# Six output-gate chunks moved from the scan stage into the seven-product stage, with a later start and a denser spread of the scan's steps

## The chip, the core and the metric

The kernel runs on one core of a Trainium2 chip. Its engines are TensorE (PE; its weight loads are PEld), VectorE (DVE), ScalarE (ACT), GpSimd (POOL) and SyncE (SP), whose queue issues every DMA here. The metric is the device time of one execution, in microseconds.

## What is computed

One step of a hybrid decoder layer over 576 tokens: 512 of a new prompt and 64 of eight running sequences. All is float32.

```
h = RMSNorm_pre(x)
[q|k|v|z_a|xBC|z_s|dt|g_a|g_s] = h @ w_in
A: sliding-window attention on q, k, v, times silu(z_a)
B: causal conv + SiLU on xBC, chunked state-space scan, gated norm with silu(z_s)
merged = sigmoid(g_a) * (A @ w_attn_br) + sigmoid(g_s) * (B @ w_ssm_br)
x <- x + RMSNorm_post(merged @ w_out)
```

The change concerns the two gates `g_a` and `g_s`, each of 2048 features. They are needed only at the very end (`merged`), so their products with `w_in` can stand anywhere before that.

## The kernel before

Activations are held transposed: 16 tiles of 128 features by 576 tokens, each as a high and a low part (`XH`, `XL`), so that one float32 product is three matmuls of 288 columns (`xh,wh`, `xl,wh`, `xh,wl`). A chunk is 128 output features. Its weights are two units of 128x1024 (tile `wr`). `split_w` (L329, L330) turns a unit into `wh` (a cast on ACT) and `wl` (a subtraction on DVE). `wr`, `wh` and `wl` have three buffers each.

A chunk is computed in one of two ways. `dense` (L345, its matmuls are L365) takes 16 k-tiles x 2 halves x 3 = 96 matmuls. `Strassen` takes chunks in pairs: seven products of 8 x 3 = 24 matmuls, 168 for a pair where `dense` has 192, with four additions of weight units on DVE and seven splits in place of four. Its matmuls are L164 to L166.

The stages stand in this order:

- 2b: the projections for z_a, z_s and xBC as pairs. The list `ch` gives the chunks, `pairs` joins them two by two.
- 3: `dense` chunks for k, v, q. The attention runs beside them in the background.
- 4: `dense` chunks for the gates. The scan (branch B) runs beside them in the background.
- 5: the two branch products and the output product, four `dense` chunks and then pairs in each phase.
- 6: the rest of the output product and the final norm.

Background work is a Python generator; each `yield` ends a step. `dense` calls `pump` 16 times in a chunk, each time adding `self.rate` to a credit, and runs one step for each whole credit. In stage 4 the rate is `R4` = 1.08, so a chunk carries 17.28 steps. `master` in stage 4 goes through eight groups of the scan. In each, `prompt(g)` (four pieces of 128 tokens: `d_front`, `d_back`), `sample(g)` (the 64 sample tokens: `e_front`, `e_back`) and `tail(g - 1)` (the gated norm of the group before, `d_norm`) are interleaved step by step. A group has 60 steps.

Code order is not the order on an engine. The framework's scheduler places each engine's instructions by its own model of when they can start, earlier code first, so scan steps that are late in code order come ahead of chunks that are ready. Stage 4's pools also take over memory of stage 3's, so the first load of the scan waits until the attention's last store has left.

Two small pieces of the scan are touched as well. In `e_front` eight ACT instructions (L1393) form relu(a - x) for eight heads, each 64x64. In `e_stack` ACT casts one operand twice to two partition ranges (L1405 and L1406, L1410 and L1411).

Of the kernel before, what the change touches and what calls it, by code (L numbers as in the profile page):

```python
# [13 lines left out]
AF = mybir.ActivationFunctionType  # L14
ALU = mybir.AluOpType
# [3 lines left out]
P = 128  # L19
# [3 lines left out]
TS = 64  # L23
T = TP + TS
TH = T // 2
# [6 lines left out]
SG = 8  # L32
# [5 lines left out]
Z_A, Z_S, G_A, G_S, KK, VV, QQ, XBC = 0, 16, 48, 64, 80, 84, 88, 104  # L38
# [54 lines left out]
NZ0 = 6  # L93
L_CV = 3 + TP + 11 * NB
HK = UK // 2
R4 = 1.08
NB0 = 4
NO1 = 12
TSP = 384
# [169 lines left out]
class Prog:  # L269
# [188 lines left out]
    def run(self):  # L458
        nc, io, tc = self.nc, self.io, self.tc
# [7 lines left out]
        for jj in range(4):  # L467
            for c in [KK + jj, VV + jj] + [QQ + 4 * jj + i for i in range(4)]:
                pl += win(c)
        for c in list(range(G_A, G_A + 16)) + list(range(G_S, G_S + 16)):  # L470
            pl += win(c)
        units = lambda w, c: [io[w][2 * c], io[w][2 * c + 1]]
        for w, o in (("wat", 0), ("wss", 0), ("wss", 16), ("wo", 0)):
# [269 lines left out]
    def stage2b(self, s2):  # L743
        nc, io = self.nc, self.io
# [9 lines left out]
        def z_out(dst):  # L754
# [7 lines left out]

            return dest, fin

        def conv_out(m):
            def dest():
                s = self.t(p, (P, L), "cs", bufs=2)
# [35 lines left out]
        ch = []  # L803
# [3 lines left out]
            ch.append((Z_S + c, z_out(self.d_zs[c])))  # L807
        for m in range(NCONV):
            ch.append((XBC + m, conv_out(m)))
        w = io["win"]  # L810
        pairs = []
        for (a, ea), (b, eb) in zip(ch[0::2], ch[1::2]):
# [88 lines left out]
    def stage3(self, s3):  # L901
# [97 lines left out]
        for jj in range(4):  # L999
            self.dense(k_evac(jj), raw=self.raw)  # L1000
            self.dense(v_evac(jj), raw=self.raw)
            for h in range(2):
# [3 lines left out]
                    if h == 0 and c == 0:  # L1006
                        v_tail(jj)
                ready[0] = j + 1
        for c in range(2):
            self.dense(self.g_evac(self.d_ga[c]), raw=self.raw)  # L1010
        self.drain()

# [159 lines left out]
    def stage4(self, s4):  # L1172
# [18 lines left out]
        def tail(g):  # L1191
            if g >= 0:
                yield from self.d_norm(g)
            if g + 2 < SG:
                self.group_load(g + 2)
            yield

        def master():
            self.G, self.AT, self.E2 = {}, {}, {}
            self.group_load(0)  # L1200
            self.at_load(0, 0)
            self.ats_load(0)
            yield
            for g in range(SG):
                a = prompt(g)
                yield from rr([a, sample(g), a, tail(g - 1)])
            yield from tail(SG - 1)

        self.bg.append(master())
        self.rate = R4  # L1210
        for c in range(2, 16):
            self.dense(self.g_evac(self.d_ga[c]), raw=self.raw)
        for c in range(15):
            self.dense(self.g_evac(self.d_gs[c]), raw=self.raw)
        p = self.p4
        first = self.t(p, (P, 4, T), "xs", bufs=2)
# [13 lines left out]

        for k in range(6):
            load(k)
        self.dense(self.g_evac(self.d_gs[15]), hook=take, raw=self.raw)
        self.drain()

    def group_load(self, g):
# [119 lines left out]
    def e_front(self, g, st):  # L1356
# [31 lines left out]
        nc.vector.tensor_mul(cbm[0:TS, 0:TS], cb[0:TS, 0:TS], self.bdt)  # L1388
        bts = st["bts"] = self.t(p, (TS, P), "bts", bufs=1)
        nc.scalar.copy(bts, cb[0:TS, P : 2 * P])  # L1390
        for i in range(8):
            ah = self.at[0:TS, 4, h8.start + i : h8.start + i + 1]
            nc.scalar.activation(ats[:, i], ats[:, i], AF.Relu, bias=ah, scale=-1.0)  # L1393
        nc.scalar.activation(ats, ats, AF.Exp, scale=-1.0)
        yield
        nc.vector.tensor_tensor(ats, ats, cbm[0:TS, 0:TS].unsqueeze(1).broadcast_to([TS, 8, TS]), ALU.mult)
# [2 lines left out]
    def e_stack(self, u, st):  # L1399
        nc, p = self.nc, self.p4  # L1400
        us = slice(32 * u, 32 * u + 32)
        xdf = st["xdes"].rearrange("p h d -> p (h d)")
        bts = st["bts"]
        x3 = self.t(p, (96, TP), "x3", F32R, bufs=2)
        nc.scalar.copy(x3[0:32], xdf[us])  # L1405
        nc.scalar.copy(x3[32:64], xdf[us])  # L1406
        nc.vector.tensor_sub(x3[64:96], xdf[us], x3[us].bitcast(F32))
        b3 = self.t(p, (96, P), "b3", F32R, bufs=1)
        other = slice(32 - 32 * u, 64 - 32 * u)
        nc.scalar.copy(b3[us], bts[us])  # L1410
        nc.scalar.copy(b3[64:96], bts[us])  # L1411
        nc.vector.tensor_sub(b3[other], bts[us], b3[us].bitcast(F32))
        bm = self.t(p, (96, 4, P), "bm", F32R, bufs=2)
        nc.vector.tensor_tensor(
            bm,
            b3.bitcast(F32).unsqueeze(1).broadcast_to([96, 4, P]),
            self.bm.unsqueeze(2).broadcast_to([96, 4, P]),
            ALU.mult,
        )
        return x3, bm  # L1420
# [447 lines left out]
```

## Time and profile before

| | |
|---|---|
| median of three runs | 3005.59 us (3004.52 to 3009.65) |
| the profiled execution | 3007.05 us, of which the span of the trace is 3005.3 us |
| PE busy | 2916.9 us (97%) |
| DVE busy | 2181.9 us (73%) |
| ACT busy | 1575.8 us (52%) |
| POOL busy | 347.1 us (12%) |
| mean granted TensorE clock | 0.990 |

A table of windows gives, for each stretch of the span, the time in which each engine had an instruction running, the number of instructions in brackets, the granted clock as a share of full speed, and how busy the DMA engines were. Matmuls overlap in the trace, so the time of one in a row of matmuls is the stretch divided by their count, not the duration shown for one.

### The profile page before, as it was taken

To read this page: it belongs to the slowest core of one execution; us is meant where nothing else is said; L and a number is where in the kernel's file an instruction comes from. 1 tells how busy PE (TensorE), PEld (TensorE's weight loads), DVE (VectorE), ACT (ScalarE), POOL (GpSimd) and SP (SyncE) were. 2 spreads that over 40 slices of the span, in tenths; PEclk is the share of its full clock that TensorE was granted. 3 is DMA by queue.
4 is the path that set the end of the run, shared out by engine and by line. 5 is a ranking of instruction groups with operands and counts; after the bars stand their busy time and mean duration, and the time that the engine had idled before them with its cause. 6 is when DMAs were issued, how large, how long until landed. Compare 5 with 4: busy or idle time off the path is not lost. (4 is left out here: it accounts for less than half of the span.)

```text
span 3005.3 us, 56009 instructions
## 1 busy us (share of the span) xinstructions
PE 2916.9 (97%) x21696; PEld 2829.8 (94%) x21696; DVE 2181.9 (73%) x3224; ACT 1575.8 (52%) x3163; POOL 347.1 (12%) x431
## 2 busy tenths in 40 slices
PE   8999999999999999999999699999999999999998
PEld 7999999999999999999999488888899999999997
DVE  7866666688888885666654887766767687887865
ACT  4444444455555554555555766666544454544552
POOL 1000000000000001322221443333200000000002
PEclk9999999999999999999999899999999999999998
DMA  8733333343433433333334677767675485775836
GB/s 288 245 127 126 114 128 123 117 131 114 128 126 115 136 112 115 100 100 99 97 104 157 199 238 244 248 237 234 210 242 179 156 284 179 253 236 165 261 116 237
DMA packets 233755, 512.23 MB, mean 170 GB/s; under 512 B 46857, under 2 KB 79369, under 8 KB 233233
## 3 DMA queue, kind: packets, MB, share of 16 engines
q1 hardware_dynamic: 233488, 508.66, 51.6%
q8 instruction: 170, 2.79, 0.4%
q14 instruction: 97, 0.79, 0.1%
HBM read 402.97 MB, written 109.65 MB: 171 GB/s over the span
## 5 line engine op out<-in xcount | busy, mean ns | idle before, releaser
L365 PE MATMUL pd<-xh,wh 128*128 128x288 f32 (+1 forms) x2464 | 738.1, 301 | 5.2 <-DVE raw L579 2.7
L365 PE MATMUL pd<-xl,wh 128*128 128x288 f32 (+1 forms) x2464 | 730.8, 297 | 0.0
L365 PE MATMUL pd<-xh,wl 128*128 128x288 f32 (+1 forms) x2464 | 730.5, 297 | 0.0
L164 PE MATMUL pb<-xh,wh 128*128 128x288 f32 x1608 | 476.2, 296 | 5.2 <-ACT wh L329 4.4
L166 PE MATMUL pb<-xh,wl 128*128 128x288 f32 x1608 | 476.0, 296 | 3.8 <-DVE wl L330 3.8
L365 PEld LDWEIGHTS pd<-xh,wh 128*128 128x128 f32 (+1 forms) x2464 | 460.9, 187 | 19.9 <-issue 9.1
L165 PE MATMUL pb<-xl,wh 128*128 128x288 f32 x1608 | 475.4, 296 | 0.0
L365 PEld LDWEIGHTS pd<-xl,wh 128*128 128x128 f32 (+1 forms) x2464 | 461.7, 187 | 9.8 <-issue 6.0
L365 PEld LDWEIGHTS pd<-xh,wl 128*128 128x128 f32 (+1 forms) x2464 | 461.5, 188 | 6.9 <-issue 4.8
L330 DVE TENSOR_TENSOR wl<-wr,wh 128x1024 fp32r<-128x1024 f32 (+1 forms) x276 | 336.4, 1221 | 156.1 <-ACT wh L329 150.5
L329 ACT CAST wh<-wr 128x1024 fp32r<-128x1024 f32 (+1 forms) x276 | 283.3, 1029 | 242.5 <-PE pb L165 106.7
L329 ACT CAST wh<-sx 128x1024 fp32r<-128x1024 f32 x198 | 207.8, 1050 | 282.7 <-PE pb L165 156.8
L329 ACT CAST wh<-sr 128x1024 fp32r<-128x1024 f32 x170 | 178.6, 1050 | 318.0 <-PE pb L165 240.4
L164 PEld LDWEIGHTS pb<-xh,wh 128*128 128x128 f32 x1608 | 303.1, 189 | 6.2 <-ACT wh L329 4.8
L166 PEld LDWEIGHTS pb<-xh,wl 128*128 128x128 f32 x1608 | 303.1, 188 | 4.6 <-DVE wl L330 4.6
L165 PEld LDWEIGHTS pb<-xl,wh 128*128 128x128 f32 x1608 | 303.3, 189 | 0.0
L330 DVE TENSOR_TENSOR wl<-sr,wh 128x1024 fp32r<-128x1024 f32 x170 | 208.0, 1224 | 109.0 <-ACT wh L329 108.9
L330 DVE TENSOR_TENSOR wl<-sx,wh 128x1024 fp32r<-128x1024 f32 x198 | 241.6, 1221 | 58.4 <-ACT wh L329 58.1
L164 PE MATMUL pb<-T2h,wh 128*128 128x288 f32 x536 | 158.2, 295 | 4.1 <-ACT k L173 4.1
L164 PE MATMUL pb<-T1h,wh 128*128 128x288 f32 x536 | 158.5, 296 | 0.9 <-ACT wh L329 0.8
L165 PE MATMUL pb<-T3l,wh 128*128 128x288 f32 x536 | 158.5, 296 | 0.0
L164 PE MATMUL pb<-T3h,wh 128*128 128x288 f32 x536 | 158.4, 295 | 0.0
(345 smaller groups left out, 6488.6 us busy)
## 6 DMA issues: line engine op xcount, KB each, us to landing
wr<-win SPq DMA_DIRECT2D x192, 512.0 KB
sr<-win SPq DMA_DIRECT2D x112, 512.0 KB
sr<-dso SPq DMA_DIRECT2D x64, 288.0 KB
wr<-wss SPq DMA_DIRECT2D x34, 512.0 KB
att<-dat SPq DMA_DIRECT2D x32, 512.0 KB
s<-sst SPq DMA_DIRECT2D x32, 512.0 KB
o_ss<-s SPq DMA_DIRECT2D x32, 512.0 KB
sr<-wss SPq DMA_DIRECT2D x30, 512.0 KB
```

Source lines behind the costliest of these rows:

```text
L164: mm(ps, a, xh, start=k == 0 and not cont, stop=False, skip_group_check=cont)
L165: mm(ps, a, xl, start=False, stop=False, skip_group_check=cont)
L166: mm(ps, b, xh, start=False, stop=k == UK - 1, skip_group_check=cont)
L329: nc.scalar.copy(wh[:, o : o + n], raw[:, o : o + n])
L330: nc.vector.tensor_sub(wl[:, o : o + n], raw[:, o : o + n], wh[:, o : o + n].bitcast(F32))
L365: self.nc.tensor.matmul(ps[x], wt[:, sl], xt[k][:, xs], start=k == 0 and s == 0, stop=k == KC - 1 and s == 2)
```

## The change

Three things are altered. The last six chunks of `g_s` (`NGS` = 6) leave stage 4 and the list of dense weight units; they become the last three pairs of stage 2b, with an output routine `g_out` that stores the raw product. Stage 3 ends with four chunks of `g_a` (`NG3`) where it had two. Stage 4 thus has 22 chunks where it had 30; `R4` becomes 1.49 (23.84 steps a chunk), the loads of the second group are issued with those of the first, the scan begins with ten empty steps, and in the first group the place of the norm is taken by 14 empty steps. In `e_front` and `e_stack` work goes from ACT to POOL.

```
-R4 = 1.08
+NGS = 6
+R4 = 1.49
+NG3 = 4
...
-        for c in list(range(G_A, G_A + 16)) + list(range(G_S, G_S + 16)):
+        for c in list(range(G_A, G_A + 16)) + list(range(G_S, G_S + 16 - NGS)):
             pl += win(c)
...
+        def g_out(dst):
+            def dest():
+                raw = self.t(self.rp, (P, T), "raw", bufs=2)
+                return raw, raw[:, 0:TH], [(raw[:, TH:T], slice(0, TH), same)]
+
+            def fin(raw):
+                self.st(dst, raw)
+                yield
+
+            return dest, fin
...
             ch.append((XBC + m, conv_out(m)))
+        for c in range(16 - NGS, 16):
+            ch.append((G_S + c, g_out(self.d_gs[c])))
...
-        for c in range(2):
+        for c in range(NG3):
             self.dense(self.g_evac(self.d_ga[c]), raw=self.raw)
         self.drain()
...
             if g >= 0:
                 yield from self.d_norm(g)
-            if g + 2 < SG:
+            else:
+                for _ in range(14):
+                    yield
+            if 0 <= g < SG - 2:
                 self.group_load(g + 2)
             yield
...
             self.ats_load(0)
-            yield
+            self.group_load(1)
+            for _ in range(10):
+                yield
...
-        for c in range(2, 16):
+        for c in range(NG3, 16):
             self.dense(self.g_evac(self.d_ga[c]), raw=self.raw)
-        for c in range(15):
+        for c in range(15 - NGS):
             self.dense(self.g_evac(self.d_gs[c]), raw=self.raw)
...
-        self.dense(self.g_evac(self.d_gs[15]), hook=take, raw=self.raw)
+        self.dense(self.g_evac(self.d_gs[15 - NGS]), hook=take, raw=self.raw)
...
-        for i in range(8):
-            ah = self.at[0:TS, 4, h8.start + i : h8.start + i + 1]
-            nc.scalar.activation(ats[:, i], ats[:, i], AF.Relu, bias=ah, scale=-1.0)
+        nc.gpsimd.tensor_tensor(
+            ats, self.at[0:TS, 4, h8].unsqueeze(2).broadcast_to([TS, 8, TS]), ats, ALU.subtract
+        )
+        nc.scalar.activation(ats, ats, AF.Relu)
...
-        nc.scalar.copy(x3[32:64], xdf[us])
+        nc.gpsimd.tensor_copy(x3[32:64], x3[0:32])
...
-        nc.scalar.copy(b3[64:96], bts[us])
+        nc.gpsimd.tensor_copy(b3[64:96], b3[us])
```

The order of instructions moves in three places. The first is PE at the start of the scan, about 40 gate matmuls behind its first transpose. L1330 (L1350 in the changed kernel) is the scan's first state product; L365 (L367) is a gate matmul; L1348, L1451, L1454, L1284 and L1322 are scan matmuls. Before:

```order
L365 MATMUL pd_19990<-xh_58_395,wl_19999 128x288
L1330 MATMUL pb_18830<-xde_18695,bt_18737 128x512
L1294 MATMUL pb_18847<-C_18666,B_18665 128x128
L1295 MATMUL pb_18847<-cst_72,B_18665 128x128
L1348 MATMUL pb_18871<-att_18673,xdt_18693 64x128 x8
L1451 MATMUL pb_18918<-sh_18892,cm_18648 128x512
L1454 MATMUL pb_18926<-x_2690_18882,bm_18890 128x512
L1284 MATMUL pb_18942<-cst_72,xs_18664 128x128 x4
L1322 MATMUL pb_18971<-C_18666,S_18832 128x128 x4
```

The rows go on like this, without one gate matmul, through the whole first group and the first half of the second. The same place in the changed kernel:

```order
L367 MATMUL pd_20366<-xh_44_367,wl_20375 128x288
L1350 MATMUL pb_19757<-xde_19649,bt_19691 128x512
L1314 MATMUL pb_19776<-C_19575,B_19574 128x128
L1315 MATMUL pb_19776<-cst_72,B_19574 128x128
L367 MATMUL pd_20367<-xh_44_367,wh_20374 128x288
L367 MATMUL pd_20367<-xl_45_368,wh_20374 128x288
L367 MATMUL pd_20367<-xh_44_367,wl_20375 128x288
L367 MATMUL pd_20366<-xh_46_371,wh_20374 128x288
```

Gate matmuls now stand between the scan's in the whole first group: from the first transpose to the norm of that group PE meets 236 of them, where it met 44 before.

The second place is DVE in the middle of stage 4, where L330 (L332) is the subtraction that finishes a weight unit and every other row is the scan's. Before, two such rows have eight others between them:

```order
L330 TENSOR_TENSOR wl_22148<-wr_21878,wh_22147 128x1024
L1488 TENSOR_TENSOR xs_21036<-xs_21036,z_22028 128x576
L1407 TENSOR_TENSOR x_3199_22103<-xdes_21930,x_3199_22103 32x512
L1297 TENSOR_TENSOR cbm_22062<-pb_22059,cst_72 128x128
L1407 TENSOR_TENSOR x_3221_22220<-xdes_21930,x_3221_22220 32x512
L1311 TENSOR_TENSOR att_21895<-att_21895,cbm_22062 128x512 x2
L1412 TENSOR_TENSOR b_3200_22107<-bts_21984,b_3200_22107 32x128
L1351 TENSOR_TENSOR xs_21880<-pb_22092,xs_21880 128x4x128
L1414 TENSOR_TENSOR bm_22111<-b_3200_22107,cst_72 96x512
L330 TENSOR_TENSOR wl_22288<-wr_22040,wh_22287 128x1024
```

In the changed kernel, at the start of the second group:

```order
L332 TENSOR_TENSOR wl_21093<-wr_20837,wh_21092 128x1024
L1488 TENSOR_TENSOR xdes_20240<-pb_20231,xdes_20240 64x512
L1371 TENSOR_TENSOR xs_19573<-pb_20247,xs_19573 128x4x128
L1502 TENSOR_TENSOR xs_19573<-pb_20290,xs_19573 128x4x64
L1306 TENSOR_TENSOR xdt_20314<-pb_20309,dt_13566 128x512
L1308 TENSOR_TENSOR xde_20316<-pb_20309,dec_13600 128x512
L1509 TENSOR_TENSOR xs_19573<-xs_19573,z_20243 128x576
L1509 TENSOR_TENSOR xs_19573<-xs_19573,z_20245 128x576
```

The next such row in the changed kernel is the 49th behind the one shown. Five of the eight groups have a stretch of this kind, 36 to 49 rows long.

## Rows read from the trace of the kernel before

**Rows 1.** Windows of stage 4: length, busy of each engine, clock, DMA share, GB/s.

```profile
1640.00:2190.00 550.00, 509.02 (x3671) 441.39 (x3670) 404.80 (x592) 350.51 (x900) 192.02 (x143) 0.98 0.69 231
1640.00:1740.00 100.00, 70.50 (x438) 51.57 (x437) 80.93 (x121) 74.73 (x205) 39.12 (x31) 0.88 0.69 217
1740.00:2190.00 450.00, 438.52 (x3236) 389.82 (x3235) 323.87 (x472) 275.78 (x695) 152.90 (x113) 1.00 0.69 234
```

**Rows 2.** Windows of the gate matmuls alone (L365): length, PE, PEld, clock, DMA share.

```profile
1640.00:1740.00 100.00, 18.14 (x116) 15.95 (x115) 0.88 0.69 217
1740.00:2190.00 450.00, 325.82 (x2094) 290.33 (x2093) 1.00 0.69 234
```

**Rows 3.** Windows of 20 us at the start of the scan, columns as in rows 1.

```profile
1640.00:1660.00 20.00, 12.88 (x95) 11.18 (x94) 11.44 (x20) 18.24 (x54) 0.92 (x1) 0.89 1.04 335
...
1700.00:1720.00 20.00, 13.49 (x73) 8.09 (x73) 16.66 (x26) 17.74 (x47) 11.39 (x9) 0.83 0.27 86
1720.00:1740.00 20.00, 17.66 (x118) 14.77 (x119) 16.50 (x21) 10.47 (x25) 9.13 (x7) 1.00 0.80 227
```

**Rows 4.** Waits of PE from 1636 to 1760 us: total, times, longest.

```profile
PE pb L1330 <- ACT bt L1299: 10.2, 1, 10.2
PE pb L1451 <- ACT sh L1432: 6.7, 2, 5.4
```

**Rows 5.** Timeline of SP's queue at the start of the scan: start, duration, what is issued.

```profile
1628.07 0.33 SPq L292 DMA_DIRECT2D wr<-win  x1
...
1634.60 0.33 SPq L292 DMA_DIRECT2D B<-dxc  x1
...
1654.78 1.69 SPq L292 DMA_DIRECT2D wr<-win  x2
...
1737.25 0.40 SPq L292 DMA_DIRECT2D wr<-win  x1
```

**Rows 6.** Timeline of PE: the scan's first transpose, and stage 5's first seven-product matmul.

```profile
1640.65 0.27 PE L1284 MATMUL pb<-cst,xs 128*128 128x128 f32 x1
...
2268.90 0.29 PE L164 MATMUL pb<-xh,wh 128*128 128x288 f32 x1
```

**Rows 7.** Windows of stage 2b, columns as in rows 1.

```profile
300.00:325.00 25.00, 25.00 (x191) 25.00 (x190) 17.45 (x17) 11.49 (x16) 0.00 (x0) 1.00 0.34 121
...
1100.00:1125.00 25.00, 25.00 (x191) 25.00 (x190) 18.50 (x28) 15.51 (x33) 0.20 (x2) 1.00 0.32 110
```

**Rows 8.** Groups of DVE by line, 1640 to 2190 us: busy, mean ns, idle before.

```profile
L330 DVE TENSOR_TENSOR wl<-wr,wh 128x1024 fp32r<-128x1024 f32 x46 | 59.2, 1287 | 52.9 <-ACT wh L329 52.9
L1311 DVE TENSOR_TENSOR att<-att,cbm 128x512 f32<-128x512 f32 x64 | 53.8, 865 | 11.7 <-ACT att L1305 10.8
L1433 DVE TENSOR_TENSOR sl<-s,sh 128x512 fp32r<-128x512 f32 x64 | 53.4, 842 | 8.0 <-ACT sh L1432 4.5 <-PE pb L1348 3.4
```

**Rows 9.** One line of DVE each: ns shortest/median/longest, starts.

```profile
L1311 DVE TENSOR_TENSOR att<-att,cbm x48: 676/684/1920, 1761.3 to 2158.0; 128x512 f32<-128x512 f32 x48
...
L1433 DVE TENSOR_TENSOR sl<-s,sh x64: 673/681/2111, 1658.3 to 2158.6; 128x512 fp32r<-128x512 f32 x64
```

**Rows 10.** A group of POOL, 1640 to 2190 us, columns as in rows 8.

```profile
L1436 POOL TENSOR_TENSOR s<-s,es 128x512 f32<-128x512 f32 x64 | 75.0, 1175 | 158.4 <-DVE sl L1433 151.1 <-DMA e<-de 6.5 <-DMA o_ss<-s 0.8
```

**Rows 11.** Groups of ACT, 1640 to 2190 us, columns as in rows 8.

```profile
L1393 ACT ACTIVATE ats<-ats,at 64x64 f32<-64x64 f32 x64 | 17.3, 337 | 23.5 <-DMA ats<-dats 19.7 <-PE pb L1284 3.8
...
L1406 ACT CAST x<-xdes 32x512 fp32r<-32x512 f32 x16 | 9.9, 618 | 0.3
...
L1394 ACT ACTIVATE ats<-ats 64x512 f32<-64x512 f32 x8 | 5.0, 624 | 0.0
L1411 ACT CAST b<-bts 32x128 fp32r<-32x128 f32 x16 | 4.7, 296 | 0.4
```

**Rows 12.** Waits of ACT from 1740 to 2190 us: total, times, longest.

```profile
ACT e L1307 <- DMA e<-de: 44.6, 12, 5.7
ACT att L1303 <- DMA att<-dat: 43.4, 12, 9.0
```

## The prediction

> **What bounds the kernel now.** I read the page's summary first: PE is busy for 97% of the span, so only what shortens PE's work or its gaps can move the end. Then I took windows of the stages that the change touches. In stage 2b PE has no gap: 191 matmuls in every 25 us, 0.1309 us each, with DVE busy 17 to 18 of 25 us [rows 7]. Stage 4 is different. Over 1740 to 2190 us PE is busy 438.5 of 450 us, so 11.5 us are gaps. In the 100 us before that it is busy 70.5, and the granted clock is 0.88 [rows 1]. Only 116 gate matmuls run in those 100 us [rows 2], which is 15.2 us of work at the pace of stage 2b.
>
> So the second thing to see is a hole at the start of the scan. PE walks through nearly two groups of the scan almost bare, as the order shows, and waits for what ACT and DVE have not yet made: 10.2 us once for ACT, 6.7 us for casts of the states [rows 4]. The weight queue says the same from its side: after the loads at 1654.78 us the next weight unit is issued at 1737.25 us [rows 5]. The clock is at 0.83 to 0.89 of full speed (a mix of its levels 1.2 and 2.4 GHz) in the windows where PE is busy 13 of 20 us, and at 1.00 where it is busy 17.7 [rows 3].
>
> How big is the hole? In the 450 us behind it run 2094 gate matmuls [rows 2], 274.1 us. Less these and the 11.5 us of gaps, 164 us are left for about 6.1 groups of the scan: 27 us of PE for a group. The hole holds 15.2 us of gate work and 1.9 groups, 51 us; the other 33 to 34 us are lost.
>
> From the scan's first transpose to the first seven-product matmul of stage 5 the stage takes 628.3 us [rows 6]. The order has 2780 gate-type matmuls in between (the four plain chunks of stage 5 included): 363.9 us, and the scan is 8 x 27 = 216 us. So 48 us in all are lost there: about 33 in the hole, 11.5 in the middle, some 4 at the end.
>
> **The change, part by part.**
>
> *Six chunks become three pairs.* 576 matmuls leave stage 4 (75.4 us) and 3 x 168 = 504 come to stage 2b (66.0 us). That is 9.4 us less PE work. In stage 2b each pair brings DVE seven splits and four additions, of about 1.2 us each, and the joins, as every pair there does; PE had no gap with 17.5 of 25 us of DVE [rows 7], so I cost this at nothing. The pairs before the end carry the convolution's work on top, and the new pairs carry its remainder; there too PE had no gap with 18.5 us. If that cover failed, a split would come late by its own 1.2 us, at most some 4 us for a pair.
>
> *The start of the scan.* By the order 676 dense matmuls stand between the last q chunk and the first transpose in both kernels, so the two chunks given to stage 3 cost nothing: they ran in the attention's shadow before. What the ten and fourteen empty steps change is how far the scan lags behind the code order when it starts. The first group now has gate matmuls between its own, so PE has work while the first loads and casts come. I take the hole of 33 us as gone in this form. The waits for the first loads remain for ACT, but PE has 236 gate matmuls (31 us) to cover them up to the first norm.
>
> *The compression.* This is what speaks against the change. Eight groups now have to run beside 1772 gate matmuls (221.5 a group, 29.0 us); another 432 (56.5 us) stand behind the last norm. PE's own work per group is 29.0 + 27 = 56.0 us. DVE in the stage is busy 404.8 us [rows 1]; its 46 weight subtractions [rows 8] take about 56 of that, so the scan needs 349 us. With some 40 subtractions left (49 us), DVE needs 398 us of the 448 us that PE needs: 89%, where it was 72% in the middle of the stage and 81% in the hole [rows 1].
>
> What a group then takes I bound from two rows. From below: PE alone, 56.0 us. From above: in the hole, with 58 gate matmuls to a group, a group took 50 us, and behind it, with 343, some 74 us; the straight line between the two gives 63.8 us at 221.5. It is an upper bound as long as a group takes the longer of two times, the scan's own pace and PE's work, since such a curve lies below its chord. I take the middle, 59.9 us, because the stretches without a weight subtraction (36 to 49 DVE instructions, 25 to 35 us) are about as long as PE's work beside them, and each should cost a few us of waiting. The stage is then 8 x 59.9 + 56.5 + 4 = 540 us, where it was 628.3.
>
> *ACT work to POOL.* ACT loses 64 small relus (17.3 us) and 32 copies (about 15 us) and gains eight relus of some 0.62 us [rows 11]: 27 us less on an engine that is busy 64% of the stage [rows 1]. PE's end gets nothing from that; it shortens the chain that DVE waits on. POOL gains 40 instructions. The trace shows neither form there; from below they cost what ACT's rows show (0.3 to 0.6 us), from above the 1.18 us of POOL's two-input row [rows 10]. I take the upper price for the 24 larger ones: about 33 us of POOL in the stage.
>
> Does that slow DVE? The row shows a cost: the same multiplication takes 0.68 us in the median, 1.92 at worst and 0.865 on average; the state subtraction 0.68, 2.11 and 0.842 [rows 8, 9]. For these two lines, 128 instructions, that is 22 us above the median. With the lines not shown I put it at some 29 us, beside 192 us of POOL, so 0.15 us for each us of POOL, and 5 us of DVE for the new work. The Trainium skill ("SBUF — State Buffer", section "SBUF: two separate sides") says that a GpSimd instruction and a VectorE instruction with two SBUF inputs hold their shared ports exclusively, and that the later one waits for the whole of the earlier. The longest times in the row agree with that. By the rule at its worst all of POOL's new 33 us would stop DVE. I count the row's 5 us, inside the middle value; what the rows' longest times would make of it is a rival below.
>
> **Sum.** Stage 4: 540 - 628.3 = -88 us; stage 2b: +66 us. Together -22 us. Against the profiled execution (3007.05 us, of which 1.75 us lie outside the span) that is 2985 us. The median of the runs is 1.5 us lower, so against it 2984. I say 2985.
>
> **The rivals.**
>
> *The cover is complete.* If DVE keeps ahead by the three finished weight units that it can hold, a group takes PE's 56 us and only the gaps of the old middle remain, about 1.9 us a group. Stage: 8 x 57.9 + 60.5 = 524 us, -38 us in all: 2968. For it: PE lost 11.5 of 450 us with scan and gates interleaved [rows 1]. Against it: DVE had 28% to spare there and has 11% now.
>
> *The hole moves instead of closing.* The scan still has its bare stretches, one in five of the groups, and loses about as much in them as the hole did. Then only the 9.4 us of saved matmuls are left, with the old 48 us of loss: 2997. For it: those stretches in DVE's order. Against it: in the hole two such stretches stood behind each other and behind cold loads.
>
> *The scan sets the end, and the kernel is slower.* The place is the norm of a group: its single row goes through the same two buffers as the gate chunks' results, so a gate chunk waits for it when the scan lags, and the scan lags wherever its loads are late. ACT waited 88 us for `e` and `att` in the middle of stage 4 [rows 12], 14 us a group, at no cost so far because PE had gate work. If a group takes 66 us the stage is 8 x 66 + 60.5 = 588.5 and the sum +26 us: 3033. It decides from 62.7 us a group on, where the stage's 562.3 us and the 66 us of stage 2b make 628.3. For it: DVE at 81% use, as in the hole, would need 62 us. Against it: that hole contains 16 us in which DVE did 11.4 us of work at most, behind cold loads [rows 3].
>
> *POOL holds DVE up in full.* The longest times, 1.92 and 2.11 us against 0.68 [rows 9], are more than one POOL instruction [rows 10] above the median. If each new one did that, DVE would lose 33 us instead of 5 and need 53.9 us a group. That is 60.6 us at 89% use and 62.7 at 86%; at 62 us the sum is 6 us below the old time: 3001.
>
> **How the numbers follow.** The forecast with its own spread (57.5 to 62 us a group, 2966 to 3002) has 0.50. The complete cover has 0.17, the moved hole 0.10, the slower scan 0.15, POOL in full 0.08. Two runs of this kernel are told apart by about 0.2%, 6 us. Faster by more than that: nearly all of the first two and of the moved hole, 0.74. Within it: the upper edge of the forecast and POOL in full, 0.11. Slower: 0.15. The range goes from 2958 (under the complete cover) to 3016, where a group takes the 63.8 us of the chord.
>
> **What would show it.** Right: three more pairs at the end of stage 2b at 191 matmuls in 25 us; no window of 20 us at the scan's start under 17 us of PE, and a clock of 1.00 there; first transpose to first seven-product matmul of stage 5 in about 540 us; DVE at 85 to 90% in between. Wrong: PE gaps of 10 us or more at the chunk borders behind each norm, or a stage of over 562 us; DVE lines with two SBUF inputs at a mean well above 0.87 us would point to POOL, and waits of ACT for `att` and `e` that PE shares would point to the loads.

## The result and the profile after

The changed kernel takes 3037.09 us (median of four runs, 3031.01 to 3042.66), the kernel before in the same series 3005.06 us (3001.33 to 3009.65). The ratio is 1.0105, with a 95% interval of 1.0091 to 1.012: slower by 1%. The forecast was 2985 us and the range ended at 3016, so both the sign and the range were wrong.

The profiled execution took 3038.17 us with a span of 3036.4 us. Stage 4, from the scan's first transpose (1711.40 us) to stage 5's first seven-product matmul (2301.58 us), takes 590.2 us. It took 628.3 us before [rows 6], so it became 38 us shorter; 540 us were forecast. The page of the changed kernel numbers its lines 2 to 21 higher: L367 is the gate matmul (L365 before), L332 the weight subtraction (L330), L1331 and L1454 the scan's multiplication and state subtraction (L1311, L1433).

Windows of the changed kernel, cut at the last norm's reduction: length, then busy time of PE, PEld, DVE, ACT and POOL, granted clock, DMA share, GB/s.

```profile
1711.40:2226.70 515.30, 456.97 (x3237) 388.22 (x3235) 416.76 (x583) 313.94 (x790) 226.92 (x183) 0.95 0.68 234
2226.70:2301.58 74.88, 64.04 (x435) 62.24 (x433) 52.16 (x95) 37.19 (x71) 9.20 (x1) 0.88 0.73 243
```

The same two windows for the gate matmuls alone (PE, PEld, clock, DMA share, GB/s):

```profile
1711.40:2226.70 515.30, 268.70 (x1773) 246.60 (x1772) 0.95 0.68 234
2226.70:2301.58 74.88, 63.45 (x432) 62.16 (x432) 0.88 0.73 243
```

And the kernel before, cut at the same marks:

```profile
1640.65:2188.15 547.50, 506.52 (x3655) 439.19 (x3653) 404.80 (x592) 348.94 (x898) 192.02 (x143) 0.98 0.69 231
2188.15:2268.90 80.75, 79.67 (x593) 78.67 (x592) 57.77 (x101) 41.86 (x78) 1.80 (x1) 1.00 0.77 256
```

A group of the scan took 547.5 / 8 = 68.4 us before and takes 515.3 / 8 = 64.4 us now. PE is idle for 58 of the 515 us, where it was idle for 41 of 547.5. DVE is busy 81% of the stretch, up from 74%. Behind the last norm, 432 gate matmuls (56.5 us at 0.1309) take 74.9 us: 18 us are lost there, against 3 before (591 matmuls, 77.4 us).

Where PE waits now is told by windows of 20 us of the changed kernel (columns as above), to be held beside [rows 3]:

```profile
1720.00:1740.00 20.00, 20.00 (x149) 17.68 (x147) 19.01 (x28) 17.51 (x44) 11.09 (x10) 1.00 0.89 314
1740.00:1760.00 20.00, 20.00 (x158) 17.12 (x155) 19.62 (x28) 11.77 (x27) 12.53 (x11) 1.00 0.82 288
1760.00:1780.00 20.00, 10.49 (x70) 9.00 (x71) 13.84 (x20) 15.50 (x43) 6.06 (x6) 0.84 0.47 159
1780.00:1800.00 20.00, 16.67 (x83) 10.26 (x83) 17.72 (x27) 11.60 (x32) 11.04 (x9) 0.74 0.26 92
...
1840.00:1860.00 20.00, 14.30 (x65) 9.90 (x65) 19.75 (x31) 14.08 (x40) 9.97 (x10) 0.83 0.20 72
...
2240.00:2260.00 20.00, 9.67 (x42) 8.69 (x43) 6.72 (x11) 3.45 (x7) 1.92 (x1) 0.66 0.78 252
```

The scan's start is closed, at a clock of 1.00. The holes stand 50 us later, and again every 80 to 120 us: PE does 10 to 17 of 20 us, in instructions of the scan, and the clock falls to 0.74. In such a window DVE is busy up to 19.75 of 20 us, or it waits itself, for ACT and for loads.

The longest waits of PE from 1690 to 2340 us (total, times, longest), which answer to [rows 4]:

```profile
PE pb L1350 <- DVE xde L1308: 12.2, 6, 2.7
PE pb L1525 <- POOL z L1514: 10.0, 1, 10.0
PE pb L1350 <- ACT bt L1319: 9.5, 1, 9.5
PE pd L367 <- ACT xh L742: 9.0, 2, 7.8
```

The 9.5 us for `bt` are the old wait of 10.2 us, in another place (it now ends at 1777.89 us). The 10.0 us for `z` are one wait, at the sum of squares of the last norm; the kernel before has no wait of 3 us or more there. The norm's chain over DVE, ACT and POOL, with a late load of `z` in it, stands bare in PE's order (start, us, what ended the idle time):

```profile
2222.16 0.76 DVE L1509 TENSOR_TENSOR xs<-xs,z 128x576 f32<-128x576 f32 x1 [4.28 <-DMA z<-dzs]
2225.28 1.12 PE L1525 MATMUL pb<-z,one 128*1 128x288 f32 x2 [9.98 <-POOL z L1514]
```

The last line of the waits is the end of the stage. Last, groups of DVE by line, 1711 to 2230 us (busy, mean ns, idle before), beside [rows 8]:

```profile
L1331 DVE TENSOR_TENSOR att<-att,cbm 128x512 f32<-128x512 f32 x64 | 59.5, 954 | 5.3 <-ACT att L1325 5.0
L1454 DVE TENSOR_TENSOR sl<-s,sh 128x512 fp32r<-128x512 f32 x64 | 56.8, 898 | 2.1 <-ACT sh L1453 2.0
L332 DVE TENSOR_TENSOR wl<-wr,wh 128x1024 fp32r<-128x1024 f32 x37 | 52.9, 1430 | 27.6 <-ACT wh L331 25.1 <-DMA xs<-dxc 1.5 <-PE pb L1315 0.8
```

Every one of them takes longer than before (954 for 865 ns, 898 for 842, 1430 for 1287). The prediction had named such means as the sign of POOL; the first experiment asks whether that is so.

### The profile page after: what moved, and what is told of

The parts are those of the page before. It is cut to its first block, busy times and chain, and to the rows that moved or that the text cites. A ratio compares the mean times of both kernels' runs of the same rounds, so it can differ in the third digit from the quotient of the medians.

```text
span 3036.4 us, 55921 instructions
## 1 busy us (share of the span) xinstructions
PE 2920.7 (96%) x21624; PEld 2831.6 (93%) x21624; DVE 2232.0 (74%) x3254; ACT 1564.9 (52%) x3084; POOL 389.3 (13%) x471
## 5 line engine op out<-in xcount | busy, mean ns | idle before, releaser
L367 PE MATMUL pd<-xh,wh 128*128 128x288 f32 (+1 forms) x2272 | 675.9, 299 | 12.5 <-ACT xh L742 9.0
L367 PE MATMUL pd<-xl,wh 128*128 128x288 f32 (+1 forms) x2272 | 677.1, 298 | 1.9 <-DVE xl L743 1.9
L367 PE MATMUL pd<-xh,wl 128*128 128x288 f32 (+1 forms) x2272 | 674.3, 298 | 0.0
L166 PE MATMUL pb<-xh,wh 128*128 128x288 f32 x1680 | 497.0, 296 | 6.3 <-DVE raw L180 2.5
L168 PE MATMUL pb<-xh,wl 128*128 128x288 f32 x1680 | 496.8, 296 | 1.8 <-DVE wl L332 1.8
L167 PE MATMUL pb<-xl,wh 128*128 128x288 f32 x1680 | 496.4, 295 | 0.0
L367 PEld LDWEIGHTS pd<-xh,wh 128*128 128x128 f32 (+1 forms) x2272 | 426.3, 188 | 21.9 <-ACT xh L742 9.5
L367 PEld LDWEIGHTS pd<-xl,wh 128*128 128x128 f32 (+1 forms) x2272 | 427.0, 188 | 8.3 <-issue 2.7
L367 PEld LDWEIGHTS pd<-xh,wl 128*128 128x128 f32 (+1 forms) x2272 | 427.1, 188 | 5.6 <-issue 2.7
L332 DVE TENSOR_TENSOR wl<-wr,wh 128x1024 fp32r<-128x1024 f32 (+1 forms) x268 | 331.4, 1239 | 127.7 <-ACT wh L331 120.0
L332 DVE TENSOR_TENSOR wl<-sr,wh 128x1024 fp32r<-128x1024 f32 x178 | 217.9, 1224 | 114.1 <-ACT wh L331 114.0
L332 DVE TENSOR_TENSOR wl<-sx,wh 128x1024 fp32r<-128x1024 f32 x207 | 252.8, 1222 | 60.8 <-ACT wh L331 60.3
L168 PE MATMUL pb<-T2h,wl 128*128 128x288 f32 x560 | 165.7, 296 | 0.0
```

The source lines that it names most:

```text
L166: mm(ps, a, xh, start=k == 0 and not cont, stop=False, skip_group_check=cont)
L167: mm(ps, a, xl, start=False, stop=False, skip_group_check=cont)
L168: mm(ps, b, xh, start=False, stop=k == UK - 1, skip_group_check=cont)
L332: nc.vector.tensor_sub(wl[:, o : o + n], raw[:, o : o + n], wh[:, o : o + n].bitcast(F32))
L367: self.nc.tensor.matmul(ps[x], wt[:, sl], xt[k][:, xs], start=k == 0 and s == 0, stop=k == KC - 1 and s == 2)
```

## The experiments

Theory A in the expectations: DVE's work, not PE's, limits the pace of a group, so taking gate chunks out of stage 4 gives back little of their time and is a loss by itself. Its rivals: the POOL forms hold DVE up; the higher rate or the empty steps do harm; the loss sits in the last norm and its loads.

Each ratio is to the runs of the kernel before in the same series; their medians lie between 3004.08 and 3008.16 us. "Lost" in the table is the stretch from the first transpose to the last norm, less 216 us for the scan's own PE work (the prediction's 8 x 27) and 0.1309 us for each gate matmul in it; the tail is what follows up to stage 5, and its loss is counted in the same way. All of it but the times and ratios is from the profiled executions, which can lie some us beside the median of their kernel (e5 and e11 7 us above it, e10 6), so a few us between two rows tell nothing. In "lost" is PE's wait at the last norm's sum, where a kernel has one: 10.0 us in the changed kernel, 13.5 in e1, 10.3 in e4, 11.0 in e6, 10.8 in e9, and nothing of 3 us or more in the others.

| kernel | time, us | ratio to before [95%] | gate matmuls a group | us a group | lost | DVE busy | tail | lost there |
|---|---|---|---|---|---|---|---|---|
| before | 3005.06 | 1 | 274 | 68.4 | 45 | 74% | 80.8 | 3 |
| changed | 3037.09 | 1.0105 [1.0091, 1.012] | 222 | 64.4 | 67 | 81% | 74.9 | 18 |
| e1 | 3041.63 | 1.0128 [1.0108, 1.0148] | 222 | 65.5 | 76 | 78% | 75.1 | 19 |
| e2 | 3002.25 | 0.9996 [0.9985, 1.0008] | 289 | 67.8 | 24 | 80% | 74.6 | 14 |
| e3 | 3006.12 | 1.0002 [0.999, 1.0014] | 270 | 66.2 | 31 | 79% | 75.6 | 19 |
| e4 | 3048.06 | 1.0152 [1.0128, 1.0177] | 186 | 62.9 | 93 | 81% | 98.6 | 4 |
| e5 | 3038.09 | 1.0107 [1.0087, 1.0126] | 216 | 64.2 | 71 | 80% | 84.1 | 15 |
| e6 | 3037.47 | 1.0099 [1.0081, 1.0117] | 222 | 64.7 | 69 | 81% | 75.4 | 19 |
| e7 | 3000.71 | 0.9978 [0.9962, 0.9993] | 222 | 60.5 | 36 | 82% | 72.4 | 16 |
| e8 | 2992.18 | 0.9948 [0.9931, 0.9965] | 277 | 67.0 | 29 | 78% | 79.3 | 6 |
| e9 | 3062.96 | 1.0194 [1.018, 1.0208] | 222 | 67.5 | 92 | 85% | 74.8 | 18 |
| e10 | 2991.39 | 0.9957 [0.9944, 0.997] | 276 | 66.8 | 29 | 78% | 81.2 | 6 |
| b124 | 3024.70 | 1.0063 [1.005, 1.0077] | 240 | 64.6 | 50 | 78% | 124.1 | 5 |
| e11 | 3004.85 | 0.9998 [0.9987, 1.0008] | 258 | 65.3 | 37 | 81% | 99.0 | 5 |

**e1: the changed kernel with ScalarE's forms back.**

```diff
-        nc.gpsimd.tensor_tensor(
-            ats, self.at[0:TS, 4, h8].unsqueeze(2).broadcast_to([TS, 8, TS]), ats, ALU.subtract
-        )
-        nc.scalar.activation(ats, ats, AF.Relu)
+        for i in range(8):
+            ah = self.at[0:TS, 4, h8.start + i : h8.start + i + 1]
+            nc.scalar.activation(ats[:, i], ats[:, i], AF.Relu, bias=ah, scale=-1.0)
...
-        nc.gpsimd.tensor_copy(x3[32:64], x3[0:32])
+        nc.scalar.copy(x3[32:64], xdf[us])
...
-        nc.gpsimd.tensor_copy(b3[64:96], b3[us])
+        nc.scalar.copy(b3[64:96], bts[us])
```

> The changed kernel with the ACT forms of e_front and e_stack back in place; everything else as changed. If the new POOL work is what makes the kernel slower (VectorE instructions with two SBUF inputs wait for it), VectorE's lines L1331 and L1454 go back from 0.95 and 0.90 us to about 0.87 and 0.84, some 20 us of VectorE are free, and the time falls to about 3015 us. If the density of the scan and the end of stage 4 are the cause, it stays within 6 us of the changed kernel's 3037.

It is no faster: 1.0128 against 1.0105, intervals that overlap. DVE does get 9 us back (407.8 for 416.8 us busy), most of it in small lines beside the former POOL work, and the stretch is 9 us longer all the same, 3.5 of them in the wait at the last norm. The two lines of the expectation did not go back at all:

```profile
L1331 DVE TENSOR_TENSOR att<-att,cbm 128x512 f32<-128x512 f32 x64 | 59.1, 953 | 4.3 <-ACT att L1325 4.1
L1453 DVE TENSOR_TENSOR sl<-s,sh 128x512 fp32r<-128x512 f32 x64 | 56.6, 893 | 7.1 <-ACT sh L1452 7.0
```

So their longer means do not come from the new POOL work (e5, which has none of it, shows 962 and 925 ns). The new POOL work is not the cause of the loss.

**e2: the scan's start alone; all gate chunks stay in stage 4.**

```diff
-NGS = 6
-R4 = 1.49
+NGS = 0
+R4 = 1.17
```

> No chunk goes to stage 2b (NGS = 0) and the rate is 1.17, so that the scan's code again ends in the last chunk; the empty steps, the four early chunks and the POOL forms stay. If the later start closes the hole of 33 us and only the missing cover of six chunks costs time, this one is the fastest yet: 8 groups at 65 to 69 us, some 15 to 25 us lost in the last chunk, 2985 us. If the hole only moves into the bare stretches (there is one in most groups of its order, 31 to 35 VectorE instructions long), about 3003, no change.

No change from before: 0.9996. But the loss in the scan's stretch halves, 45 to 24 us, and 10 us of that come back as loss in the tail. Its stretch:

```profile
1641.70:2184.20 542.50, 517.64 (x3779) 458.03 (x3777) 433.97 (x595) 328.90 (x814) 238.36 (x183) 0.98 0.68 236
```

**e3: two chunks moved instead of six.**

```diff
-NGS = 6
-R4 = 1.49
+NGS = 2
+R4 = 1.27
```

> Two chunks go to stage 2b in place of six (NGS = 2, rate 1.27). By the density theory the loss per group lies between the two: 8 groups at 65 to 66 us, the last chunk as in the changed kernel, 3005 to 3012 us. If the loss of the changed kernel were a matter of the start or of the last chunk alone, the missing 3.1 us of matmuls a pair would be all that differs: 3043.

Between e2 and the changed kernel in pace (66.2 us) and loss (31 us), and no faster than before. Each chunk that leaves adds to the loss, and not all alike: by the medians the first two cost 4 us against e2, the next four 31.

**e4: the changed kernel with a higher rate.**

```diff
-R4 = 1.49
+R4 = 1.75
```

> The changed kernel with a rate of 1.75 in place of 1.49: the scan's code ends after 18 of 22 chunks, so the last norm no longer falls into the chunk that loads stage 5's operands. If that chunk costs about 30 us, they come back, but the order again has a stretch of 86 VectorE instructions without a weight subtraction at the start, as before the change, which costs 20 to 33: 3025 to 3040 with a last chunk without gaps. If the last chunk's gaps come from somewhere else, they stay and the time rises to 3055 or more.

The windows of its scan and tail:

```profile
1706.60:2209.80 503.20, 430.73 (x2949) 354.88 (x2948) 406.39 (x577) 306.03 (x778) 232.17 (x183) 0.92 0.67 231
2209.80:2308.36 98.56, 97.33 (x723) 96.48 (x721) 61.54 (x105) 46.05 (x85) 1.80 (x1) 0.99 0.68 231
```

The 3048.06 us lie between the two ranges that were expected. With the last norm a few chunks ahead of the end, the tail loses 4 us instead of 18. The scan's stretch loses 93: 36 fewer gate matmuls a group (4.7 us of PE) shorten a group by 1.5 us only.

**e5: the kernel before with only the six chunks as pairs.** `g_out`, the list `ch` and the shorter loops as in the change; nothing else of it (so ScalarE's forms too, as in e1), except that the rate rises from 1.08 to 1.38, since 24 chunks now carry the steps of 30. Against the changed kernel:

```diff
-R4 = 1.49
-NG3 = 4
+R4 = 1.38
...
-            self.group_load(1)
-            for _ in range(10):
-                yield
+            yield
```

> The kernel before with only the six chunks moved to stage 2b as three pairs (rate 1.38, so that the scan's code ends as far from the end as before); no empty steps, two early chunks, the ACT forms. Theory A (the scan's pace: VectorE cannot be used beyond about 81% next to PE, so a group takes 62 to 64 us whatever gate work is left beside it): the stage shrinks by less than the 66 us that stage 2b grows, 3030 to 3045 us, so moving the chunks is a loss by itself. Rival B (the start and the last chunk make the loss, and both came with the empty steps and the rate of 1.49): about 2996.

The whole loss is there already: 1.0107. Over the stretch the scan loses 71 us with its start open, where the changed kernel loses 67 with it closed. The start of e5:

```profile
1700.00:1720.00 20.00, 7.79 (x41) 5.89 (x41) 6.55 (x14) 10.90 (x39) 1.00 (x1) 0.71 0.85 278
1720.00:1740.00 20.00, 14.37 (x77) 9.78 (x73) 17.28 (x26) 17.32 (x43) 8.55 (x7) 0.77 0.63 215
1740.00:1760.00 20.00, 14.58 (x90) 10.24 (x90) 18.36 (x28) 12.01 (x36) 11.36 (x10) 0.83 0.78 252
1760.00:1780.00 20.00, 11.09 (x56) 7.71 (x56) 16.89 (x29) 19.37 (x56) 7.52 (x6) 0.74 0.25 88
```

PE does 48 of these 80 us, and 67 of the 80 from 1720 us in the changed kernel: 19 us are gained at the place, and 4 are left at the end of the stretch. Of the others 10 are the wait at the last norm, which e5 does not have.

**e6: the last group's row on another queue.**

```diff
-        self.st(d[1].rearrange("(p c) -> p c", p=TS), r)
+        q = nc.gpsimd if g == SG - 1 else nc.sync
+        q.dma_start(d[1].rearrange("(p c) -> p c", p=TS), r)
...
-        self.ld(rs, d[1:2].broadcast_to([P, T]))
+        q.dma_start(rs, d[1:2].broadcast_to([P, T]))
```

> The changed kernel with one edit: in the last group the row's store and its broadcast load are issued by GpSimd instead of SyncE. In the changed kernel SyncE's queue stood at that store for 8 us, waiting for a GpSimd instruction of 9.2 us, and the loads of stage 5's operands were behind it. If this block makes the gaps of the last chunk (18 us behind the last norm where the kernel before had 3), 8 to 15 us come back: 3022 to 3029. If the operand loads are late because the scan ends late, whatever the queue, less than 5 us: 3033 to 3038.

No gain. The branch operands that were queued on SP behind the row's store (2241.95 us) are loaded some 4 us earlier, and then DVE stands in the norm's multiplication, waiting for the row, with the operand's subtraction behind it:

```profile
2250.56 3.01 DVE L1545 SCALAR_TENSOR_TENSOR xs<-xs,par,z 128x576 f32<-128x576 f32 x4 [6.67 <-DMA z<-drs]
```

The wait moved from SP's queue to DVE's. It belongs to the last norm standing near the end of the stage: in the table the kernels with 562 or more gate matmuls behind that norm lose 3 to 6 us there, those with 528 or fewer 14 to 19.

**e7: less DVE work in the norm.** The kernel leaves the row's factor out of the output.

```diff
-            nc.vector.scalar_tensor_tensor(xs[:, f], xs[:, f], gc, rs, ALU.mult, ALU.mult)
+            nc.scalar.activation(xs[:, f], xs[:, f], AF.Identity, scale=gc)
```

> The changed kernel with the last multiplication of the gated norm on ScalarE, without the row's factor (that factor is left out of the output). VectorE loses 4 instructions of 0.98 us a group, 31 us in the stage. Theory A (VectorE at 80% sets the pace): a group gets 4.9 us shorter until PE's own 56 us bind, the stage 25 to 39 us, 2998 to 3012. Rival C (the chain of waits between the engines, not VectorE's load, sets the pace): less than 10 us, 3027 or more.

Its stretch:

```profile
1709.50:2193.80 484.30, 447.44 (x3238) 388.06 (x3236) 397.57 (x555) 330.37 (x822) 227.17 (x183) 0.97 0.75 251
```

DVE has 19 us less to do and the stretch is 31 us shorter, at the same gate and scan matmuls. It is the largest effect of any edit, and it is not pure: 10 of the 31 us are the wait at the last norm, which is gone, DVE also no longer waits for the row and less for the norm's loads of `z` (17.7 us for 29.0), and ACT takes the work. So e9 asks the opposite with nothing else changed.

**e9: more DVE work that nothing waits for.**

```diff
+            dm = self.t(p, (P, 64), "dm", bufs=1)
+            for _ in range(6):
+                nc.vector.tensor_tensor(dm, self.ident[:, 0:64], self.ident[:, 0:64], ALU.add)
             nc.vector.tensor_mul(xs[:, f], xs[:, f], z[f])
```

> The changed kernel with DVE work added that nothing waits for: 24 additions of 128x64 ahead of the norm's row multiplications of each group, 192 in all, into a tile that nobody reads; nothing is left out. Their length is not in the rows; between 0.1 and 0.25 us each, they are 19 to 48 us of DVE in the 515 us before the last norm. Theory A (DVE's share of busy time, about 80% in all runs so far, sets the pace of a group): the stretch up to the last norm grows by at least what DVE gets, 1.0 to 1.3 us for each us added, so 20 to 60 us, and the time is 3057 to 3095. Theory C (the chains of waits through the scan set the pace, and DVE has 98 us of idle time in this stretch to take work in): the stretch grows by less than a third of what is added, and the time is 3040 to 3050.

Its stretch and the part of it in which the additions stand, then the added line itself (ns shortest, median, longest; first and last start):

```profile
1710.10:2249.70 539.60, 462.45 (x3238) 390.90 (x3236) 459.69 (x761) 314.09 (x790) 226.42 (x183) 0.94 0.65 223
...
1710.00:1944.00 234.00, 198.53 (x1352) 165.42 (x1352) 223.86 (x432) 142.68 (x365) 98.89 (x81) 0.93 0.62 215
```

```profile
L1511 DVE TENSOR_TENSOR dm<-cst x192: 203/224/2339, 1704.1 to 1944.0; 128x64 f32<-128x64 f32 x192
```

and the same line as a group in the part (busy, mean ns):

```profile
L1511 DVE TENSOR_TENSOR dm<-cst 128x64 f32<-128x64 f32 x178 | 58.8, 330 | 2.9
```

The time is in Theory A's range (3062.96; the other theory's ended at 3050), but the price is not: DVE is busy 43 us longer and the stretch grew by 24, so 0.57 us for each us. The additions themselves take 58.8 us, while the other DVE instructions take 16 us less than in the changed kernel; for each us that was added it is 0.41. That is far from the 1.0 to 1.3 of Theory A and somewhat above the third of the other. The scheduler set the additions ahead of their place in the code, all before 1944 us, into DVE's gaps as far as it could; there DVE is busy 96% of the time. So 0.4 to 0.6 is what a us of DVE costs where the scheduler put it. POOL waited 10.1 us for the additions, which may be a part of that. DVE limits a part of the scan, not all of it.

**e8, e10, e11 and b124: the better half of the change.** e8 keeps all gate chunks in stage 4 (as e2) and takes a rate of 1.24; e10 is e8 with ScalarE's forms as in e1; e11 is e8 at a rate of 1.31; b124 is the kernel before with its rate alone raised.

```diff
-NGS = 6
-R4 = 1.49
+NGS = 0
+R4 = 1.24
```

> No chunk moved (NGS = 0), rate 1.24 in place of the 1.17 of the earlier run without moved chunks, so that the scan's code ends some two chunks before the stage's end. The run at 1.17 lost 24 us beside the scan and 14 behind the last norm. If the 14 come from the scan's end falling into the last chunk, 8 to 10 of them go, and the middle may give back a few: 2990 to 2998, faster than the kernel before. If it only shifts the loss into denser groups: 3000 to 3005.

> The kernel with empty scan steps, ten more early loads, all sixteen gate chunks in stage 4 and two more of the early ones as in the changed kernel, at rate 1.24 (2992.18 us with the three GpSimd forms), now with ScalarE's own forms of before in place of the GpSimd ones. If the GpSimd forms pay where the scan's pace is set by DVE and gate matmuls together, 2994 to 3001; if they cost DVE its shared port, as the long means of DVE's multiplications let one think, 2984 to 2990; if they matter for nothing, within 3 us of 2992.

> The kernel with empty scan steps and all sixteen gate chunks in stage 4, at rate 1.31 in place of 1.24. A group then has fewer gate matmuls beside it (about 262 in place of 277), and by the slope of 0.047 us a matmul measured so far it is 0.7 us shorter, 5.6 us over eight groups; some 120 gate matmuls more are left for behind the last norm, 15.7 us at 0.1309. Theory A: 3.0 to 4.5 us lost in the stretch up to the last norm by PE's missing work is only regained if the tail loses less; it loses 5.7 us now and can regain 3 at most, so the time is 2994 to 3002. If the end of the stage still costs more than its 5.7 us show, 2984 to 2991.

> The kernel before with one number changed: the rate at which scan steps are taken between gate matmuls, 1.08 to 1.24. None of the change's parts is in it. If the gain of the best kernel so far (13 us) comes from the rate alone, 2990 to 2996; if the hole at the start of the scan (about 33 us) stays and moves with the rate as it is, the end of the scan comes earlier and its last chunk goes without cover no longer, the time is 3000 to 3012; the theory that the empty steps and the higher rate only work together says 2999 to 3012.

e8 beats both kernels: 0.9948 [0.9931, 0.9965], 16 us below the kernel before in its series (3008.16). Its stretch and tail:

```profile
1640.20:2175.80 535.60, 503.27 (x3684) 444.60 (x3682) 420.09 (x593) 326.46 (x810) 231.85 (x183) 0.98 0.69 236
2175.80:2255.05 79.25, 77.42 (x565) 76.31 (x563) 55.92 (x99) 40.01 (x75) 1.80 (x1) 0.98 0.77 261
```

e10 is level with it (0.9957 [0.9944, 0.997]), so the POOL forms matter for nothing here either. e11 came out at the upper end of 2994 to 3002 and a little beyond (3004.85): more of stage 4 lies behind the scan than its shorter groups gain. Of the 15 us between the profiled executions of e11 and e10, 6 stand in stage 4 (its stretch and tail take 621.6 us, e10's 615.2), 3.5 ahead of the first transpose and 5 behind stage 4; why, I can't say.

b124 was the surprise: every expectation allowed 2990 to 3012 and it took 3024.70. The rate alone opens the start of the scan a little further (PE does 36 of the 60 us below, 39 in the kernel before), and PE waits 6.8 us for the first load just ahead of the first transpose, where the kernel before waits less than 1 us. First the windows of b124 there, then those of e8, at the same rate but with the empty steps and two more early chunks:

```profile
1640.00:1660.00 20.00, 7.82 (x39) 5.45 (x39) 8.92 (x17) 15.60 (x50) 0.00 (x0) 0.59 1.02 339
1660.00:1680.00 20.00, 16.36 (x68) 10.48 (x68) 19.19 (x29) 16.52 (x44) 11.72 (x10) 0.81 0.48 172
1680.00:1700.00 20.00, 12.08 (x90) 8.80 (x90) 18.73 (x32) 14.36 (x46) 8.09 (x7) 0.87 0.77 250
```

```profile
1640.00:1660.00 20.00, 20.00 (x153) 18.48 (x153) 15.76 (x23) 19.02 (x52) 6.22 (x7) 1.00 1.04 352
1660.00:1680.00 20.00, 20.00 (x136) 17.21 (x135) 19.64 (x28) 14.67 (x37) 12.95 (x10) 1.00 0.78 270
1680.00:1700.00 20.00, 17.62 (x151) 15.72 (x149) 18.21 (x29) 10.99 (x31) 8.38 (x7) 1.00 0.89 281
```

PE does 36 of 60 us in b124 and 58 in e8, 21 us of difference; the losses of the two stretches (50 and 29) differ by as much. So the closed start is worth 21 us when all gate chunks are there to cover the scan, and at the rate of 1.24 the kernel gains only with it. e8 is not without the hole further on: from 1700 to 1720 us PE does 11.45 of 20 us, with the same wait for `bt` (9.6 us).

## Why the prediction was wrong

The miss is 53 us (3038.17 measured in the profiled execution, 2985 forecast). By its own steps:

1. *Six chunks as three pairs, +66.0 us, at nothing for DVE.* Nearly right. The scan starts at 1711.40 us, 70.75 later than before, so some 5 us dearer than the sum. Most of stage 2b has its 191 matmuls in 25 us, and one window shows a gap of 1.8 us (columns as above); the rest of the 5 us is not placed:

```profile
1125.00:1150.00 25.00, 23.19 (x176) 22.95 (x175) 17.99 (x19) 11.21 (x17) 0.00 (x0) 1.00 0.39 132
...
300.00:325.00 25.00, 25.00 (x191) 25.00 (x190) 17.19 (x16) 11.49 (x17) 0.00 (x0) 1.00 0.32 118
```

2. *The hole of 33 us at the start goes.* Right at its place, too large as a gain. PE does 20.00 of 20 us there. With all chunks in stage 4 the loss falls by 21 us (before to e2, b124 to e8). With six chunks gone 19 us are gained at the place and 4 are left at the end of the stretch (e5 against the changed kernel, 71 and 67); 10 of the others are the wait at the last norm, and the rest is not placed. The new hole 50 us later is no sign of missing gate matmuls alone, since e8 has it with all of them. That was the rival "the hole moves"; it had 0.10 and a price without any further loss, which was too low.

3. *The compression: 59.9 us a group.* **This is the step that failed.** A group takes 64.4 us, 4.5 more, 36 us in eight; 10 of the 36 are the one wait at the last norm, and without it a group takes 63.2. I chose the middle between PE's own time and the chord; nothing in the rows favoured the middle, and the groups run close to the chord's 63.8. Its left end was loose too: with the 1.9 groups that I counted in the hole elsewhere (61 matmuls and 52.6 us a group, not 58 and 50) it gives 64.7. What the runs show: from 186 to 289 gate matmuls a group (e4, changed kernel, e2) a group grows from 62.9 to 67.8 us, 0.047 us a matmul (0.060 without the wait at the last norm in the first two), where PE needs 0.1309. A chunk of 96 that leaves stage 4 therefore shortens it by some 4.5 us and costs 84 x 0.1309 = 11 us as half a pair in stage 2b. Six such chunks are a loss of 39 us; from e2 to the changed kernel the span grew by 37.9 (2998.5 to 3036.4). That is no test of the slope, which is drawn through the same runs, and the line is not straight: for two chunks it gives 13 us, and from e2 to e3 the span grew by 8.7. e5 says it without the slope: 576 matmuls, 75.4 us of PE, left stage 4 of the kernel before, and the stage became 30.8 us shorter (628.3 to 597.5).

4. *DVE at 85 to 90%.* It was 81%, with PE at 89%. DVE's work was 416.8 us where I had counted 398, but it stood in 515 us and not in 448. Neither engine is near its limit on average, since in one stretch DVE sets the pace (19.75 of 20 us at 1840) and in another PE does. One reading fits the slopes: PE limits a third to a half of the scan (0.047 to 0.060 of 0.1309), and DVE about as much (0.41 to 0.57 in e9). It is argued from these slopes, not shown.

5. *The end of the stage, 4 us.* It was 18: the last norm falls into the last chunk, whose hook also loads and casts the branch operands. e4 and e8, which reach the last norm earlier, lose 4 and 6 us. This term is the other 14 us of the miss: 5, 36 and 14 make 55, and behind stage 4 the changed kernel is 2 us shorter.

6. *POOL costs DVE 5 us.* It costs about 9 in e1's comparison; the end moves by nothing that can be told. The means over 0.87 us that I had named as the sign of POOL came true and did not mean it: with the new POOL work taken out (e1) the two lines stay at 0.95 and 0.89.

The rival that came true in its price is "the scan sets the end": 66 us a group and 3033 us, deciding from 62.7. It had 0.15. Its place is only once the one it named. The waits of ACT for `e` and `att`, 78 us over the stretch, are no longer than before [rows 12]. At the last norm PE waits 10 us for a chain with a late load in it; at the others it waits in the scan's own products, and moving the last row to another queue (e6) changed nothing. DVE waits 29.0 us for the norms' loads of `z`, where it waited 9.1 before; what these 20 us cost no run shows. "The cover is complete" is refuted by the holes, "POOL holds DVE up in full" by e1.

What stays open: how much of e7's 21 us besides the last norm is DVE's 19 us of work and how much the waits for the row and for `z`; and the 8.5 us that e11 loses outside stage 4.

## What to carry to other kernels

Before work that hides a latency-bound stage is moved away, measure what the stage gives back for each unit of it: here a third to a half of the unit's own time, less than it cost elsewhere, although the same work got cheaper by an eighth. Ask the profile for the neighbours' engines in short windows and not only on average: 81% of DVE over a stage was full in some windows and waiting in others, and both showed as holes of PE. A bound drawn between two stretches of one trace is as good as the count at both its ends, and as long as nothing but the quantity on its axis differs between them.

## What the runs showed of the hardware

A small POOL instruction can be held far beyond one instruction of DVE. The norm's power of a 64x9 tile takes 1.8 us five times, 2.25 us twice and 9.2 us at the end of the stage (9.87 us there in e6), while DVE goes without a gap through subtractions with two SBUF inputs. The line's durations (ns shortest, median, longest), the instruction, and what DVE did (start, us):

```profile
L1536 POOL TENSOR_TENSOR rs_v<-rs_v,mhalf x8: 1800/1808/9196, 1804.8 to 2232.7; 64x9 f32<-64x9 f32 x8
```

```profile
2232.73 9.20 POOL L1536 TENSOR_TENSOR rs_v<-rs_v,mhalf 64x9 f32<-64x9 f32 x1 [7.50 <-DVE rs_v L1535]
```

```profile
2232.56 0.74 DVE L743 TENSOR_TENSOR xl<-B,xh 128x576 fp32r<-128x576 f32 x1
...
2238.38 1.21 DVE L332 TENSOR_TENSOR wl<-wr,wh 128x1024 fp32r<-128x1024 f32 x1
2239.51 0.74 DVE L743 TENSOR_TENSOR xl<-C,xh 128x576 fp32r<-128x576 f32 x1
2247.26 0.76 DVE L743 TENSOR_TENSOR xl<-raw,xh 128x576 fp32r<-128x576 f32 x1 [7.00 <-ACT xh L742]
```

DVE's string ends at 2240.25 us and POOL's instruction at 2241.93, one of its normal lengths later. The Trainium skill ("SBUF — State Buffer", section "SBUF: two separate sides") says that the two engines lock their shared ports for a whole instruction and that the other one fully blocks; the trace agrees, and shows besides that the one blocked did not get its turn between the nine DVE instructions that followed. No run tried the end of the stage without them.
